# First blocks of x turned by matrix products with a diagonal, and pool matrices multiplied earlier, in a hybrid attention and pooling layer

## The chip, the core and the metric

The kernel runs on one core of a Trainium2 chip. The metric is the device time of one execution in microseconds. The core's engines are TensorE (PE for its products, PEld for its weight loads), VectorE (DVE), ScalarE (ACT), GpSimd (POOL) and SyncE (SP), which here issues almost all DMA transfers. Each engine works through its own instructions in order and waits for the others by semaphores.

## What is computed

One layer of a bidirectional encoder on x of 4096 tokens by 1024 features, in float32:

```python
h = rmsnorm(x, pre_norm_g)
proj = h @ w_in                    # q | k | v | g_a | u_p | g_p
a = banded_attention(q, k, v, rel_bias, sink) * silu(g_a)   # 8 heads, |i-j| <= 128
p = multiscale_pool(u_p, pool_w, pool_scale) * silu(g_p)    # 4 groups of 128 channels
x = x + rmsnorm(concat(a, p) @ w_out, post_norm_g)
```

rmsnorm(x, g) is x / sqrt(mean(x^2) + eps) * g by rows. The pooling takes window means less the token and multiplies each group by a 128x128 matrix of pool_w; since that is linear, the kernel multiplies pool_w into the columns of w_in for u_p beforehand.

## The kernel before

The precision of float32 comes from pairs of float16 numbers: a value's high part, and a low part that is the rest. A product of two pairs is made of three float16 products. Both operands are first scaled: x by its row factor (one over the root of the mean square), a weight tile by a power of two found from its columns' norms.

The kernel has two phases, the projections (lines 200 to 1518) and attention with the output product (from line 1520). In both, every step is put into a list as `due(t, function, arguments)`. A table `later` adds an offset to single steps, the list is sorted by time, and the functions are called in that order. A manual schedule then keeps that order on each engine. So a time is not a start on the chip: it only sets which instruction stands before which in an engine's queue.

The start treats the first 512 tokens by themselves, as four blocks b = 0 to 3 of 128 rows. For each block: `x_load` brings its rows into `ybig`; `x_square` (L245 on ScalarE, L247 on VectorE) makes the sum of squares; `x_scale` (L254, L257 on GpSimd) the row factor; `x_high` (L268, ScalarE) and `x_low` (L275, VectorE) the scaled pair, into `cbig`; `x_turn` (L282) issues a transposing DMA from `cbig` to `xt`, as TensorE needs features on the partitions.

Meanwhile the first weight tiles, 0 and 2 (the gate g_p), are loaded into `raw` and squared (`w_square_raw`, L453, ScalarE). TensorE sums the squares with the squared gains `gg` as weights (`w_norm_raw`, L462; `gg` is from L413 on VectorE). `pair_scale` (L163 to L179) makes the scale. `w_fold` (L416) multiplies the gains into the tile, and `w_high` (L529) and `w_low` (L532) make its pair in `wa`.

`mm_block(si, i)` (L973) multiplies weight tile si with block i, 24 products of 128x128. Later tiles take all 512 tokens at once in `mm` (L985), 24 products each, called a0_1, a0_3, a0_8 and so on after their tile; before a0_8 stands `pair_norm` (L473), a sum of squares for tiles 8 and 10. `u_prod` (L434) multiplies the float32 columns for u_p by a pool matrix, four float32 products for each half, into a PSUM tile named wup, and `u_fold` (L442) multiplies in the gain. `row_prod` (L653) makes the bias table fp. `warm_up` (L955) is a row of products whose result nobody reads.

At the end of the second phase stand the last query blocks, 2, 1 and 0, whose attention, output product and norm alternate on all engines. Steps named below are the logits with their maximum (L1669, DVE), the exponentials (L1680, ACT), the reciprocals of the denominators (L1700, L1701, DVE), the rest of a probability pair (L1731, DVE), the join of a query tile q0_1 (L2021, DVE), and the adds of output products (L2319, DVE, into mo) that free the PSUM bank for TensorE's next product (L2277).

Of the kernel before, what the change touches and what calls it, by code (L numbers as in the profile page):

```python
# [8 lines left out]
F32 = mybir.dt.float32  # L9
F16 = mybir.dt.float16  # L10
BF16 = mybir.dt.bfloat16
# [62 lines left out]
def hybrid_layer(ctx: ExitStack, tc, io, out):  # L74
# [16 lines left out]
    nc.sync.dma_start(g_pre, io["g_pre"])  # L91
# [107 lines left out]
    with ExitStack() as actx:  # L199
# [5 lines left out]
        ones16 = pa1.tile([P, P], BF16, name="ones16")  # L205
# [46 lines left out]
        def x_scale(m, i, n=1):  # L252
            s, r = rs_t[m][:, 0, i : i + n], rs_t[m][:, 1, i : i + n]
            nc.gpsimd.tensor_scalar(  # L254
                out=s, in0=s, scalar1=D * EPS * X_SQ**2, scalar2=None, op0=ALU.add
            )
            nc.gpsimd.tensor_tensor(  # L257
                out=r, in0=s, in1=mhalf if n == 1 else mhalf.to_broadcast([P, n]), op=ALU.pow
            )
# [155 lines left out]
        def w_fold(si):  # L415
            nc.vector.tensor_tensor(out=raw_k(si), in0=raw_k(si), in1=gb, op=ALU.mult)  # L416
# [10 lines left out]
        def u_prod(j, half):  # L427

            wt = raw_of(("u", j))
            pp = psa.tile([P, 4, P], F32, name=f"wup{j}_{half}", tag="wup", bufs=3)  # L430
# [520 lines left out]
        def warm_up():  # L951

            junk = psa.tile([P, 512], F32, name="warm", tag="wup", bufs=3)
            for n in range(6):
                nc.tensor.matmul(junk, ones16, gg[:, :4], start=(n == 0), stop=(n == 5))  # L955
# [196 lines left out]
        for t, b in ((0.0, 0), (0.1, 1), (0.3, 2), (0.4, 3)):  # L1152
            due(t, x_load, b)
        for t, si in ((0.2, 0), (0.25, 2), (9.5, 1), (10.8, 3)):
            due(t, w_load, si, io["w_a"][si])
        due(20.7, lambda: nc.sync.dma_start(pw, io["pool_w"].rearrange("j p c -> p j c")))
        due(20.8, u_load, 0)
        due(20.9, u_load, 2)
        for b, (s, c, h, l) in enumerate(
            ((4.7, 5.95, 7.05, 8.15), (5.95, 7.1, 8.15, 9.4), (11.4, 12.5, 15.0, 16.4),  # L1160
             (12.5, 13.6, 17.3, 18.0))
        ):
            due(s, x_square, b, nc.vector if b == 0 else None)
            due(c, x_scale, 0, b)
# [3 lines left out]
        due(0.5, first_use)  # L1168
        due(2.0, gain_square)
        for si, s, n, f, h, l in (  # L1170
            (0, 9.25, 10.4, 11.2, 13.8, 15.1), (2, 10.3, 11.5, 13.9, 16.1, 18.9),
# [6 lines left out]
        due(12.7, pair_scale, 0)  # L1178
        due(12.9, pair_scaled, 0)
        due(20.9, pair_gate, 0)  # L1180
        due(4.0, row_load)
        due(11.7, row_prod)
        due(11.8, warm_up)
        due(21.0, row_keep)
        due(30.0, row_store)
        for t, si, i in (
            (16.3, 0, 0), (17.7, 0, 1), (19.0, 2, 0), (20.4, 2, 1), (21.7, 0, 2), (23.0, 2, 2),
# [47 lines left out]
        due(20.9, w_fold, 1)  # L1235
        due(22.2, w_square, 1)
        due(22.2, w_fold, 3)
        due(23.5, w_square, 3)
        pair_split(1, 25.0)
        for half in range(2):  # L1240
            due(27.1, u_prod, 0, half)
            due(30.5 + 0.7 * half, u_fold, 0, half)
        t = tile0(1, 29.3)
        t_first(0, 31.9)
        due(32.0, w_square, 8)
        for half in range(2):
            due(t, u_prod, 2, half)
            due(t + 1.9 + 0.7 * half, u_fold, 2, half)
        due(34.7, u_load, 1)
        due(36.4, u_load, 3)  # L1250
        due(38.0, w_square, 10)
        t = tile0(3, t + 1.9)
        t_last(0, 38.0)
        due(37.9, w_fold, 4)
# [9 lines left out]
        due(28.0, w_load_c, 4, 2)  # L1264
        due(29.0, w_load_c, 6, 3)
# [198 lines left out]
        for m in range(1, NM):  # L1464
# [28 lines left out]
            (x_turn, 0, 1): 0.4, (mm_block, 0, 3, 1): 0.8, (t_low, 0, 0, 1): 1.5,  # L1493
            (t_low, 0, 1, 1): 1.5, (t_low, 0, 3, 1): 1.5, (w_square, 4, 1): -1.5,
            (w_fold, 6, 1): -10.0, (u_fold, 1, 0, 1): -0.8, (u_fold, 1, 1, 1): -0.8,
            (u_fold, 3, 0, 1): -0.8, (u_fold, 3, 1, 1): -0.8, (w_fold_act, 12, 0, 1): 0.4,
            (w_fold_act, 13, 0, 2): 6.0, (w_fold_act, 13, 1, 2): 6.0, (q_sums, 'kv', 1): -1.5,
            (q_low, 'kv', 0, 1): 0.15, (q_high, 'kv', 1, 1): -0.8, (w_fold_act, 16, 0, 1): -10.0,
            (out_square, 1, 1): 10.0, (out_square, 4, 1): 10.0, (wo_scale, 4, 1): -0.8,
            (wo_sum1, 0, 1): -3.0, (wo_load, 1, 1): -6.0, (wo_load, 5, 1): -9.0,  # L1500
            (wo_load, 2, 1): 3.0, (wo_load, 6, 1): 3.0, (load_wo, 0, 1): 10.0, (wq_x, 1, 1): -2.2,
            (bias_head, 2, 1): 10.0, (bias_head, 5, 1): 6.0, (bias_head, 6, 1): 6.0,
            (bias_head, 7, 1): 9.0, (bias_sinks, 1): 3.0, (rs_spread, 3, 1): 8.0,
            (x_hi, 2, 'S1', 1): -10.0, (y_scale, 3, 2, 1): 10.0, (rs_row, 4, 1): 1.5,
            (rs_spread, 4, 1): 4.5, (product, 2, 1, 0, 1): -10.0, (x_hi, 4, 'A11', 1): -10.0,
            (rs_row, 5, 1): -0.8, (rs_spread, 5, 1): 5.0, (y_load, 5, 3, 1): 3.0,
            (rs_spread, 6, 1): 8.0, (x_hi, 5, 'S3', 1): -1.5, (y_scale, 6, 0, 1): 3.0,
            (x_hi, 6, 'A11', 1): -0.4, (x_hi, 6, 'A22', 1): -3.8, (x_sum, 'S3', 6): 0.8,
# [1391 lines left out]
```

## Time and profile before

| | us |
|---|---|
| median of 3 runs | 1144.49 (1143.84 to 1144.55) |
| profiled execution, its own time | 1142.67 |
| span of its instructions | 1140.9 |
| PE busy | 1110.8 (97%) |
| DVE busy | 961.1 (84%) |
| ACT busy | 725.0 (64%) |
| POOL busy | 292.5 (26%) |

Times in the profile's rows count from the start of the span. A row of a timeline has the start, the duration, the engine (PEld is the weight load, SPq SyncE's queue of DMA issues), the line of the kernel, the operation with output and input, and in brackets the idle time ahead of it with what ended that. A row of groups has the count, the busy time in total and the mean in ns, and the idle time ahead of the group. The ends of matrix products are modelled, so starts are the safer reading. The time outside the span is 1142.67 - 1140.9 = 1.77 us.

### The profile page before, as it was taken

What the parts mean: (1) busy time and instruction counts of PE and PEld (TensorE: products, weight loads), DVE (VectorE), ACT (ScalarE), POOL (GpSimd) and SP (SyncE); (2) the same over time, 40 slices, a digit from 0 to 9 for tenths busy, and PEclk for the clock granted to TensorE, in tenths of its full rate; (3) what the DMA queues carried; (4) which work ended last, traced back from release to release, by engine and by line L of the source; (5) the groups of instructions that cost most, each with busy time, mean ns of one, the idle gap of its engine ahead of it and who ended that gap; (6) DMA issues with size and microseconds to landing.
All of it is one profiled execution on the core that took longest, in us unless ns stands there. A gap on an engine that the chain in (4) does not pass through costs nothing. (4 is left out here: it accounts for less than half of the span.)

```text
span 1140.9 us, 28920 instructions
## 1 busy us (share of the span) xinstructions
PE 1110.8 (97%) x11556; PEld 816.5 (72%) x11556; DVE 961.1 (84%) x1975; ACT 725.0 (64%) x1625; POOL 292.5 (26%) x280
## 2 busy tenths in 40 slices
PE   5999999999999999999999999999999999999887
PEld 4648888888888888887567657566666666676444
DVE  6878787788878986868998888888888988988996
ACT  5856675757476545166776676676676766776573
POOL 1000000000000000001544454463454545544322
PEclk9999999999999999999999999999999999999999
DMA  9677889899998967999989998889979989889587
GB/s 258 167 252 253 218 229 290 262 262 271 277 281 204 322 217 233 353 265 261 234 203 225 203 212 210 210 187 239 211 188 225 198 192 227 211 206 198 135 187 212
DMA packets 328007, 262.02 MB, mean 230 GB/s; under 512 B 222608, under 2 KB 285712, under 8 KB 324416
## 3 DMA queue, kind: packets, MB, share of 16 engines
q1 hardware_dynamic: 323840, 245.50, 82.2%
q0 software_dynamic: 4032, 14.68, 5.2%
q8 instruction: 90, 1.47, 0.5%
q14 instruction: 45, 0.37, 0.1%
HBM read 130.87 MB, written 76.59 MB: 182 GB/s over the span
## 5 line engine op out<-in xcount | busy, mean ns | idle before, releaser
L1034 PEld LDWEIGHTS <-wa 128*128 128x128 f16 x3360 | 328.1, 98 | 39.4 <-issue 0.8
L1034 PE MATMUL ch<-xt,wa 128*128 128x256 f16 x1920 | 212.6, 273 | 0.0
L1680 ACT ACTIVATE p_all<-p_all,nm 128x385 f32<-128x385 f32 (+1 forms) x256 | 153.0, 599 | 60.8 <-DVE nm L1669 53.1
L1731 DVE SCALAR_TENSOR_TENSOR pn<-p_all,rd,pn 128x384 f16<-128x384 f32 (+1 forms) x256 | 161.5, 681 | 20.1 <-ACT pn L1723 17.4
L2277 PE MATMUL ms<-wa,ys 128*128 128x512 f16 x720 | 165.3, 379 | 2.7 <-DVE mo L2319 1.3
L1669 DVE CUSTOM_DVE_ANT_0 p_all<-s,ybig,nsink 128x385 f32<-128x385 f32 (+1 forms) x256 | 156.9, 664 | 7.1 <-PE s L1652 7.1
L1723 ACT ACTIVATE pn<-p_all,rd 128x384 f16<-128x384 f32 (+1 forms) x256 | 135.4, 596 | 5.5 <-DVE rd L1701 2.9
L2277 PE MATMUL m<-wa,y 128*128 128x512 f16 x540 | 123.9, 379 | 3.7 <-DVE mo L2319 2.1
L2277 PEld LDWEIGHTS <-ys 128*128 128x128 f16 x720 | 69.0, 98 | 79.7 <-issue 5.0
L1034 PE MATMUL cl<-xt,wa 128*128 128x256 f16 x960 | 106.4, 273 | 0.4 <-DVE cbig L1059 0.3
L2277 PEld LDWEIGHTS <-y 128*128 128x128 f16 x540 | 51.2, 98 | 64.4 <-issue 5.7
L254 POOL TENSOR_SCALAR ssq<-ssq 128x4 f32<-128x4 f32 (+1 forms) x11 | 4.0, 362 | 332.4 <-ACT jk L245 326.4
L2157 POOL TENSOR_TENSOR y<-yf,y 128x512 f16<-128x512 f32 x29 | 33.4, 1156 | 201.3 <-ACT y L2153 201.2
L2157 POOL TENSOR_TENSOR ys<-at,ys 128x512 f16<-128x512 f32 x28 | 35.6, 1272 | 131.9 <-ACT ys L2153 131.9
L346 DVE TENSOR_TENSOR xt<-ybig,xt 128x1024 f16<-128x1024 f32 x50 | 60.3, 1219 | 8.2 <-ACT xt L341 8.2
L1926 PEld LDWEIGHTS <-raw 128*128 128x128 f16 x588 | 56.7, 98 | 13.7 <-issue 1.6
L2303 ACT ACTIVATE jkb<-mo 128x512 bf16<-128x512 f32 x42 | 26.3, 626 | 63.1 <-DVE mo L2319 63.1
L1926 PE MATMUL kp<-xt,raw 128*128 128x256 f16 x540 | 65.4, 273 | 0.0
L2314 POOL TENSOR_TENSOR mo<-mo,ybig 128x512 f32<-128x512 f32 x39 | 52.4, 1342 | 44.8 <-ACT jkb L2303 44.6
L1652 PE MATMUL s<-k_all,q 64*32 64x288 f16 (+2 forms) x2856 | 60.2, 284 | 3.4 <-DVE k_all L1898 1.2
L1068 ACT ACTIVATE gp<-cbig,cg 128x256 f32<-128x256 f32 x42 | 19.0, 500 | 62.6 <-DVE cbig L1059 62.6
L1652 PEld LDWEIGHTS <-q 64*32 64x32 f16 (+1 forms) x2856 | 38.4, 92 | 27.1 <-issue 24.6
(248 smaller groups left out, 2025.3 us busy)
## 6 DMA issues: line engine op xcount, KB each, us to landing
xn<-in_x SPq DMA_DIRECT2D x28, 512.0 KB, 9.0
ybig<-in_xT SPq DMA_DIRECT2D x28, 512.0 KB, 5.4
y_scr<-xt SPq DMA_DIRECT2D x14, 1024.0 KB, 8.0
out<-mo SPq DMA_DIRECT2D x28, 512.0 KB, 5.5
xt<-y_scr SPq DMA_DIRECT2D x26, 512.0 KB, 6.2
xt<-in_x POOLq DMA_DIRECT2D x26, 512.0 KB, 4.8
xt<-x_scr SPq DMA_DIRECT2D x19, 512.0 KB, 4.6
x_scr<-xt SPq DMA_DIRECT2D x9, 1024.0 KB, 10.4
```

Source lines behind the costliest of these rows:

```text
L346: eng.tensor_tensor(out=o[:, w, 1], in0=y_view(i), in1=o[:, w, 0], op=ALU.subtract)
L1034: nc.tensor.matmul(acc[:, c], wa[:, q, wi, slot * HK + k, c * P : (c + 1) * P], x[:, xi, k, :], start=(fresh and n == 0), stop=(n > 3 * 2 ...
L1652: nc.tensor.matmul(s_bank[jj][r0 : r0 + nr, gg, lo:hi], q_t[u, half][a, qi, jj, tl + r0 : tl + r0 + nr], k_all[a, ki, k0 : k0 + hi - lo], ...
L1669: nc.vector.tensor_tensor_reduce(out=p_t[b, half][:, hh, :nk], in0=s_t[b, half][jj][:, gg, :nk], in1=bias[:, h, lo : lo + nk], scale=negc[ ...
L1680: nc.scalar.activation(p[:, hh, :nk], p[:, hh, :nk], AF.Exp, bias=nm_t[b, half][:, hh : hh + 1], scale=-1.0, accum_out=den_t[b, half][:, h ...
L1723: nc.scalar.activation(prob_view(b, half)[:, 0, i], p_t[b, half][:, i, :nk], AF.Copy, scale=rd_t[b, half][:, 0, i : i + 1],)
L1731: nc.vector.scalar_tensor_tensor(out=pn4[:, 1, i], in0=p_t[b, half][:, i, :nk], scalar=rd_t[b, half][:, 0, i : i + 1], in1=pn4[:, 0, i], o ...
L1926: nc.tensor.matmul(acc, wkv[:, slot, wi, k, :], x[:, xi, k, :], start=(onto is None and n == 0), stop=(n == 3 * HK - 1), skip_group_check= ...
L2157: eng.tensor_tensor(out=y[:, :, 1], in0=f(u), in1=y[:, :, 0], op=ALU.subtract)
L2277: nc.tensor.matmul(z_t[u, tag], y[:, k, yi, :], wo[o][:, wi, k // 2, k % 2, :], start=(n == 0 and acc is None), stop=(n == 3 * HK - 1), sk ...
L2303: nc.scalar.activation(junk, src, AF.Square, scale=2.0**-5, accum_out=ss_t[u][:, 2 * i + c : 2 * i + c + 1])
L2314: eng.tensor_tensor(out=mo, in0=mo, in1=gpost[:, cs], op=ALU.mult)
```

## The change

Blocks 0 and 1 no longer go through `cbig` and a transposing DMA. GpSimd makes a diagonal matrix of the block's row factors (`x_diagonal`, an identity `eye` times the factors, eye being a new input). TensorE multiplies each 128x128 piece of the block's float32 rows, as weights, by that diagonal (`x_cross`): the product is the piece turned and scaled, in PSUM, in tiles xc0_0, xc0_1, xc1_0, xc1_1 (block and half). ScalarE copies it to `xt` as the high part (`x_cross_high`), VectorE subtracts that for the low part (`x_cross_low`). Blocks 2 and 3 go the old way.

The pool matrices, u0, u2, w1 and w3 are loaded right after x, and the four products for u0 and u2 are made between the block products. The gains g_pre are loaded behind x1 and w0. The warm-up is the first work of TensorE, with 14 products instead of 6, and its operand is a constant instead of gg. The square of block 2 is on VectorE. The bias table is made after a0_3. In the two `later` tables many entries are new or changed.

```diff
+        def x_diagonal(b):
+            d = xc_t["d", b] = pa.tile([P, P], F32, name=f"xd{b}", tag="xd")
+            nc.gpsimd.tensor_scalar(
+                out=d, in0=eye, scalar1=rs_t[0][:, 1, b : b + 1], scalar2=None, op0=ALU.mult
+            )
+
+        def x_cross(b):
+            d = xc_t.pop(("d", b))
+            for half in range(2):
+                acc = xc_t[b, half] = (
+                    gemm.tile([P, 4, P], F32, name=f"xc{b}_{half}", tag="acc0") if b and half
+                    else psa.tile([P, 4, P], F32, name=f"xc{b}_{half}", tag="wup", bufs=3)
+                )
+                for k in range(HK):
+                    c0 = half * 512 + k * P
+                    nc.tensor.matmul(
+                        acc[:, k], ybig[:, b, c0 : c0 + P], d, start=True, stop=True
+                    )
+
+        def x_cross_high(b, half):
+            nc.scalar.copy(x_place(b, half, 0), xc_t[b, half])
+
+        def x_cross_low(b, half):
+            nc.vector.tensor_tensor(
+                out=x_place(b, half, 1), in0=xc_t.pop((b, half)), in1=x_place(b, half, 0),
+                op=ALU.subtract,
+            )
...
         def warm_up():
 
-            junk = psa.tile([P, 512], F32, name="warm", tag="wup", bufs=3)
-            for n in range(6):
-                nc.tensor.matmul(junk, ones16, gg[:, :4], start=(n == 0), stop=(n == 5))
+            junk = gemm.tile([P, T], F32, name="warm", tag="acc2")
+            for n in range(14):
+                nc.tensor.matmul(junk, ones16[:, :P], ones16, start=(n == 0), stop=(n == 13))
...
-        due(20.7, lambda: nc.sync.dma_start(pw, io["pool_w"].rearrange("j p c -> p j c")))
-        due(20.8, u_load, 0)
-        due(20.9, u_load, 2)
+        due(0.5, lambda: nc.sync.dma_start(pw, io["pool_w"].rearrange("j p c -> p j c")))
+        due(0.6, u_load, 0)
+        due(0.65, u_load, 2)
...
-        due(11.7, row_prod)
-        due(11.8, warm_up)
...
+        for n, j in enumerate((0, 2)):
+            for half in range(2):
+                due(17.5 + 0.1 * (2 * n + half), u_prod, j, half, n and half)
+                due(20.2 + 0.7 * (2 * n + half), u_fold, j, half)
+        due(36.0, row_prod)
...
         later = {
+            (x_load, 1, 1): -1.5, (w_load, 0, 1): -0.4, (u_load, 2, 1): 1.5,
```

The following rows are those of the instruction order. First SyncE at the start of the program (raw is a buffer of weights, ybig of x; in_w_uT are the columns for u_p). Before:

```order
L91 DMA g_pre_66<-in_g_pre 128x8
L235 DMA ybig_71<-in_x 128x1024 x2
L400 DMA raw_70<-in_w_a 128x1024 x2
L235 DMA ybig_71<-in_x 128x1024 x2
L647 DMA rbias_126<-in_rel_bias 32x8
L649 DMA onehot_128<-in_onehot 32x512
L400 DMA raw_70<-in_w_a 128x1024
L282 DMA_TRANSPOSE xt_72<-cbig_109 128x16x128 x2
L400 DMA raw_70<-in_w_a 128x1024
L282 DMA_TRANSPOSE xt_72<-cbig_109 128x16x128 x2
L1156 DMA pw_111<-in_pool_w 128x4x128
L400 DMA raw_70<-in_w_uT 128x1024 x2
```

The same place after the change:

```order
L234 DMA ybig_70<-in_x 128x1024
L434 DMA raw_69<-in_w_a 128x1024
L1191 DMA g_pre_66<-in_g_pre 128x8
L234 DMA ybig_70<-in_x 128x1024
L434 DMA raw_69<-in_w_a 128x1024
L1192 DMA eye_113<-in_eye 128x128
L234 DMA ybig_70<-in_x 128x1024 x2
L1195 DMA pw_110<-in_pool_w 128x4x128
L434 DMA raw_69<-in_w_uT 128x1024
L434 DMA raw_69<-in_w_a 128x1024 x2
L434 DMA raw_69<-in_w_uT 128x1024
L316 DMA_TRANSPOSE xt_71<-cbig_108 128x16x128 x2
```

The two transfers that turned blocks 0 and 1 are gone; all loads of the first products, the pool matrices included, stand ahead of the two that turn blocks 2 and 3.

VectorE at the start, from the square of block 0 to the low part of block 3. Before (cbig receives x's low parts, wa the weights'):

```order
L247 ISA jk0_130,ssq0_131<-ybig_71 128x1024
L275 SCALAR_TENSOR_TENSOR cbig_109<-ybig_71,ssq0_131,cbig_109 128x2x512 x2
L416 TENSOR_TENSOR raw_70<-raw_70,g_pre_66 128x1024
L163 TENSOR_REDUCE m2_184<-n2_0_149 128x1
...
L416 TENSOR_TENSOR raw_70<-raw_70,g_pre_66 128x1024
L532 SCALAR_TENSOR_TENSOR wa_73<-raw_70,sc_74,wa_73 128x8x128
L275 SCALAR_TENSOR_TENSOR cbig_109<-ybig_71,ssq0_131,cbig_109 128x2x512 x2
L532 SCALAR_TENSOR_TENSOR wa_73<-raw_70,sc_74,wa_73 128x8x128
```

After the change (xt receives the low parts of the tiles xc):

```order
L450 TENSOR_TENSOR raw_69<-raw_69,g_pre_66 128x1024 x2
L162 TENSOR_REDUCE m2_194<-n2_0_163 128x1
...
L246 ISA jk2_202,ssq0_149<-ybig_70 128x1024
...
L290 TENSOR_TENSOR xt_71<-xc0_0_183,xt_71 128x4x128
L569 SCALAR_TENSOR_TENSOR wa_72<-raw_69,sc_73,wa_72 128x8x128
L290 TENSOR_TENSOR xt_71<-xc0_1_188,xt_71 128x4x128
L290 TENSOR_TENSOR xt_71<-xc1_0_210,xt_71 128x4x128
L290 TENSOR_TENSOR xt_71<-xc1_1_215,xt_71 128x4x128
L569 SCALAR_TENSOR_TENSOR wa_72<-raw_69,sc_73,wa_72 128x8x128
L309 SCALAR_TENSOR_TENSOR cbig_108<-ybig_70,ssq0_149,cbig_108 128x2x512
L450 TENSOR_TENSOR raw_69<-raw_69,g_pre_66 128x1024
```

Both folds and the square of block 2 stand ahead of the first low part, and the low part of block 2 stands behind the second low part of the weights, where it stood ahead of it.

VectorE near the end of the program, at the logits of query block 1, first half (nm1_0), before:

```order
L1669 ISA p_all_5964,nm1_0_16112<-s0_5965,ybig_71,nsink_81,negc_80 128x385
L2021 TENSOR_TENSOR q0_1_16023<-kq2_7_15230,q0_1_16023 128x512
L2319 TENSOR_TENSOR mo2_1_16035<-ms1_2_16036,mo2_1_16035 128x512
...
L1700 RECIPROCAL rd1_0_16114<-den1_0_16113 128x2
L1701 TENSOR_TENSOR rd1_0_16114<-rd1_0_16114,s1_5966 128x2
L1700 RECIPROCAL rd1_0_16114<-den1_0_16113 128x2
```

And after:

```order
L1714 ISA p_all_6000,nm1_0_16148<-s0_6001,ybig_70,nsink_80,negc_79 128x385
L2364 TENSOR_TENSOR mo2_1_16071<-ms1_2_16072,mo2_1_16071 128x512
...
L1745 RECIPROCAL rd1_0_16150<-den1_0_16149 128x2
L1746 TENSOR_TENSOR rd1_0_16150<-rd1_0_16150,s1_6002 128x2
L2066 TENSOR_TENSOR q0_1_16059<-kq2_7_15266,q0_1_16059 128x512
L1745 RECIPROCAL rd1_0_16150<-den1_0_16149 128x2
```

The join of q0_1 left its place ahead of the add and stands between the two pairs of reciprocals.

More of the change, by code (lines that the diff above doesn't have):

```diff
@@ L425, in u_load, with u_prod @@
             raw_load(("u", j), io["w_uT"][j])
-        def u_prod(j, half):
+        def u_prod(j, half, spare=0):
             wt = raw_of(("u", j))
-            pp = psa.tile([P, 4, P], F32, name=f"wup{j}_{half}", tag="wup", bufs=3)
+            pp = (
+                gemm.tile([P, 4, P], F32, name=f"wup{j}_{half}", tag="acc0") if spare
+                else psa.tile([P, 4, P], F32, name=f"wup{j}_{half}", tag="wup", bufs=3)
+            )
             w_t["up", j, half] = pp
@@ L1232, in tile0 @@
             return t + SLOT
[L1235 to L1254, printed above, removed]
+        due(17.0, w_fold, 1)
+        due(19.6, w_square, 1)
+        due(18.2, w_fold, 3)
+        due(21.7, w_square, 3)
+        pair_split(1, 23.0)
+        due(24.5, w_square, 8)
+        due(27.0, w_square, 10)
+        t = tile0(1, 27.1)
+        t_first(0, 29.0)
+        due(31.0, u_load, 1)
+        due(31.1, u_load, 3)
+        t = tile0(3, t)
+        t_last(0, 34.0)
+        due(34.9, w_fold, 4)
         due(t + 1.3, w_square, 4)
@@ L1515, in hybrid_layer @@
-            (join, 7, 1, 'a', 'u2', 0, 1, 1): -1.5,
+            (pool_gate, 7, 0, 1): -0.8, (pool_store, 7, 1, 1): -1.5,
+            (join, 7, 0, 'a', 'u2', 0, 1, 1): -1.9, (join, 7, 1, 'a', 'u2', 0, 1, 1): -1.5,
         }
@@ L2888 @@
         "edge": _edge_table().reshape(64),
+        "eye": np.eye(P, dtype=np.float32),
     }
```

124 lines of the change are left out of this document (72 added, 52 removed).

## The prediction

> **What bounds the kernel now.** I first read the busy shares by stage. Each row gives the stretch, its length and the busy time of PE, PEld, DVE, ACT and POOL, with the number of instructions.
>
> ```profile
> 0.00:17.00 17.00, 6.34 (x26) 2.77 (x26) 10.61 (x18) 11.87 (x15) 4.39 (x12) 1.00 0.94 285
> 48.00:1055.00 1007.00, 1002.31 (x10575) 750.69 (x10574) 855.51 (x1761) 645.63 (x1456) 264.49 (x245) 1.00 0.90 233
> 1055.00:1141.00 86.00, 72.26 (x650) 39.18 (x648) 71.58 (x157) 47.83 (x124) 23.31 (x23) 0.98 0.71 179
> ```
>
> In the middle stretch TensorE idles 1007.00 - 1002.31 = 4.7 us out of a thousand. Nothing that only reorders VectorE, ScalarE or SyncE there can win more than that, and the diff leaves nearly all of it alone. So two questions remain: when does the product stream reach the middle, and how do the 13.7 idle us of the last stretch change? Next I read whom TensorE waits for (total, times, longest).
>
> ```profile
> PE n L462 <- ACT sq L453: 10.7, 1, 10.7
> ...
> PE gp L973 <- DMA xt<-cbig: 1.1, 1, 1.1
> ```
>
> Its start is a wait of 10.7 us for the first squared weights, and a second wait, of 1.1 us, is for the turned blocks 2 and 3. TensorE's own timeline (start, duration) shows what lies between:
>
> ```profile
> 10.66 1.96 PE L462 MATMUL n<-sq,gg 128*128 128x128 bf16 x16 [10.66 <-ACT sq L453]
> 12.55 1.87 PE L653 MATMUL fp<-onehot,rbias 32*8 32x512 f32 x2
> 14.36 2.74 PE L955 MATMUL warm<-gg,ones 128*128 128x512 bf16 x6
> 16.89 5.90 PE L973 MATMUL gp<-xt,wa 128*128 128x128 f16 x96
> 23.90 2.84 PE L973 MATMUL gp<-xt,wa 128*128 128x128 f16 x48 [1.11 <-DMA xt<-cbig]
> ...
> 29.46 2.05 PE L434 MATMUL wup<-pw,raw 128*128 128x128 f32 x16
> 31.34 5.34 PE L985 MATMUL a<-xt,wa 128*128 128x512 f16 x24
> 36.53 1.95 PE L434 MATMUL wup<-pw,raw 128*128 128x128 f32 x16
> ...
> 43.49 0.28 PE L473 MATMUL n<-wsq,ones 128*128 128x2 f32 x2
> ...
> 47.50 5.34 PE L985 MATMUL a<-xt,wa 128*128 128x512 f16 x24
> ```
>
> The first product of weight tile 8, a0_8, starts at 47.50. Both programs issue the same list from there on, so the front is worth exactly what that start moves. Two prices come from these rows. The warm-up products take (16.89 - 14.36) / 6 = 0.42 us for 512 columns; those of a0_1 take (36.53 - 31.34) / 24 = 0.216. TensorE therefore begins at half rate, and has full rate from about 17 us.
>
> **The loads.** The queue rows and the first work on x show how loads arrive.
>
> ```profile
> 0.73 0.40 SPq L91 DMA_DIRECT2D g_pre<-in_g_pre  x1
> 1.18 0.89 SPq L235 DMA_DIRECT2D ybig<-in_x  x2
> ...
> 17.61 6.03 SPq L282 DMA_TRANSPOSE xt<-cbig  x2
> ```
>
> ```profile
> 5.09 1.23 DVE L247 CUSTOM_DVE_ANT_0 jk<-ybig 128x1024 bf16<-128x1024 f32 x1 [1.44 <-DMA ybig<-in_x]
> ```
>
> ```profile
> 6.37 1.06 ACT L245 ACTIVATE jk<-ybig 128x1024 bf16<-128x1024 f32 x1 [4.15 <-DMA ybig<-in_x]
> ```
>
> Blocks 0 and 1 of x are released 1.28 us apart: one 512 KB block per 1.28 us, in order of issue. Without g_pre ahead the first block goes out at 0.73 instead of 1.18. By that spacing I estimate x1 at 4.6, w0 5.9, x0 7.2, w2 8.45, eye 8.6, x2 9.9, x3 11.1, pool matrices 11.8, u0 13.0, u2 16.9.
>
> **The work ahead of the products.** These rows carry the prices of VectorE, ScalarE and GpSimd:
>
> ```profile
> 10.98 1.22 DVE L416 TENSOR_TENSOR raw<-raw,g_pre 128x1024 f32<-128x1024 f32 x1
> 12.66 0.42 DVE L163 TENSOR_REDUCE m<-n 128x1 f32<-128x256 f32 x1 [0.46 <-PE n L462]
> ...
> 13.68 0.17 DVE L179 TENSOR_SCALAR sc<-m 128x2 f32<-128x2 f32 x1
> ...
> 16.30 1.28 DVE L275 SCALAR_TENSOR_TENSOR cbig<-ybig,ssq,cbig 128x1024 f16<-128x1024 f32 x1
> ```
>
> ```profile
> 6.74 0.57 POOL L257 TENSOR_TENSOR ssq<-ssq,mhalf 128x1 f32<-128x1 f32 x1
> ```
>
> ```profile
> L1046 ACT COPY cbig<-ch 128x512 f32<-128x512 f32 x60 | 34.1, 578 | 21.9 <-PE ch L1034 21.8
> ...
> L2157 POOL TENSOR_TENSOR y<-yf,y 128x512 f16<-128x512 f32 x29 | 33.4, 1156 | 201.3 <-ACT y L2153 201.2
> ...
> L529 ACT ACTIVATE wa<-raw,sc 128x1024 f16<-128x1024 f32 x10 | 11.3, 1138 | 1.4 <-DVE sc L179 1.4
> ...
> L442 DVE TENSOR_TENSOR raw<-wup,g_pre 128x512 f32<-128x512 f32 x8 | 5.3, 685 | 0.2
> ```
>
> ScalarE squares w0 and then w2, 1.0 us each, from 8.45 for the second; TensorE can sum them (n2_0) from 9.5 to 10.6. VectorE takes gain square at 5.95, block 0's square to 8.4, two gain folds of 1.22 to 10.8, the scale chain of 1.2 us (12.66 to 13.85 before) to 11.9, then the square of block 2 that came over from ScalarE, to 13.1. GpSimd had block 0's factor 7.31 - 6.32 = 1.0 us after its square, so now at 9.35. The diagonal is a 128x128 operation that the trace does not show. It lies between nothing and the 1.16 us of the four times larger L2157; even the upper end gives 10.5, before TensorE is free of n2_0, so it costs nothing.
>
> The turning products replace two transfers: 16 fp32 products of 128x128. The eight of L434 take 31.34 - 29.46 = 1.88, so 0.235 each and 3.8 us for all: TensorE is in them from 10.6 to 14.4. The copy out of PSUM (like L1046, 0.58) and the subtraction (like L442, 0.69) come four times each, in between the high and low parts of the weights (1.14 and 1.28). Following both queues: ScalarE has x high parts out at 12.2, 14.9, 15.4, 17.1, w0's high part from 13.25 to 14.4, w2's to 16.5. VectorE waits for 14.4, gives w0's low part at 15.6, the x low parts at 13.9, 16.2, 16.9, 17.7, w2's low part at 18.95.
>
> TensorE, from 14.4: one pool product (0.94) to 15.35, x low of block 0 is late only to 16.2, so the two 24s of weight tile 0 with a second pool product between run to 19.6; a third to 20.55, the 48 of weight tile 2 (2.85) to 23.4, the fourth to 24.35. The gate projection of blocks 0 and 1 ends 0.6 us later than before (22.79), but with all four pool products done.
>
> **The wait that is left.** Blocks 2 and 3 still go through the low part and the queue. VectorE reaches x_low of block 2 after w2's low part: 18.95 to 20.2, where it was 16.30 to 17.6. That is the late step of this change: 2.6 us. The transfer was issued at 17.61 and released TensorE at 23.90. Medians from issue to landing, and a spread with most samples, are:
>
> ```profile
> xt<-cbig SPq DMA_TRANSPOSE x4, 6.2
> ```
>
> ```profile
> vv<-vt SPq DMA_TRANSPOSE x14, 5.8
> ```
>
> ```profile
> DMA to landing us min/median/max: 4.3/6.5/10.4
> ```
>
> The third is that of wa<-pn. With the two transfers of blocks 0 and 1 gone, and fewer loads beside (w1, w3 and u are in by 17), I take 5.8, the row of single turns; bounds 4.3 and 6.5. Products of block 2 then start at 26.0 (24.5 to 26.7), a wait of 1.65 us for TensorE, where 1.1 was. All of TensorE's list queues behind that wait. On SyncE the loads of the bias table, w4, w6, u1 and u3 queue behind the two turns. The bias table is used from 41.95 on. u3 is wanted by the last pool products, at an estimated 45; it went out at 40.73 before,
>
> ```profile
> 40.73 0.33 SPq L400 DMA_DIRECT2D raw<-in_w_uT  x1
> ```
>
> when VectorE had the second low part of weight tile 1's sums. That chain now starts from n2_1 some 2 us later, but has lost four pool folds of 0.69 in between, so I keep 40.7 and take nothing; it leaves an estimated 4.3 us for the landing.
>
> Blocks 2 and 3 take 29.46 - 23.90 = 5.56, so a0_1 starts at 31.55 (31.34 before). Its weights' high part follows n2_1, at 28.85, by a chain of 1.2 and a copy of 1.14: 31.2, with 0.35 to spare. The two a0 take 5.19 each, to 41.95. The bias table's product, which was paid at half rate (1.87), now stands behind them at full rate: 0.94. Then 47.50 - 43.49 = 4.0 for the row sum and four pool products as before: **a0_8 at 46.9, or -0.6 us**, bounds -2.1 (landing after 4.3) and +0.1 (after 6.5).
>
> In short, the front hides 3.8 us of pool products and 2.5 of warm-up, saves 0.9 on the table and pays 3.8 for turning; what else it frees waits for VectorE, late with block 2.
>
> **The tail.** The last list of offsets moves few instructions. One stood on TensorE's path:
>
> ```profile
> 1081.50 0.68 DVE L2021 TENSOR_TENSOR q<-kq,q 128x512 f16<-128x512 f32 x1
> 1082.10 0.68 DVE L2319 TENSOR_TENSOR mo<-ms,mo 128x512 f32<-128x512 f32 x1
> ...
> 1085.41 0.17 DVE L1700 RECIPROCAL rd<-den 128x2 f32<-128x2 f32 x1 [0.57 <-ACT p_all L1680]
> ```
>
> ```profile
> 1082.84 2.75 PE L2277 MATMUL ms<-wa,ys 128*128 128x512 f16 x12 [1.35 <-DVE mo L2319]
> ```
>
> TensorE's 1.35 ends with the add of L2319, and the q join stood right ahead of it. It goes behind the first of the reciprocals, in the 0.57 us that VectorE waits there anyway: -0.6. ScalarE's square of a finished block leaves the middle of block 1's exponentials, after which VectorE waited 0.19: -0.2. The other swaps exchange neighbours in stretches where TensorE's next wait is set elsewhere; I take nothing for them, bounds -0.35 (ScalarE's four products of the last but one block, now ahead of a copy) and, the other way, if the q join's time is only paid later, at the reciprocals, the whole -0.8. **Tail: -0.8**, bounds -1.15 and 0.
>
> **Sum.** -0.6 - 0.8 = -1.4 us. The profiled execution took 1142.67 with a span of 1140.9; the runs had a median of 1144.49, 1.8 above it. The difference carries over: 1143.1.
>
> **Rivals.**
>
> *The turn is quick (F).* Only two turns are left in the queue, and the shortest landing of a turn was 4.3. Then the wait before block 2 all but goes, a0_8 starts at 45.4, and with the tail it is -2.1 - 0.8 = -2.9: 1141.6. Against it: the four of this very shape have 6.2 as their median. By the Trainium skill (DMA: Bandwidth & Descriptors, Latency and other measured facts) a DMA transpose moves 261 GB/s on top of about 2 us fixed; for the 512 KB of a block that is an estimate of 4.0 us, which would give this case. The row of 6.2 does not agree, with other transfers beside it.
>
> *The clock falls back (C).* The warm-up now ends near 7.1 us, and TensorE stands idle to 9.5. If the half rate of 0.42 comes back there, n2_0 still ends by 11.5, but turning takes 7.5 us, to 19, the last copy comes at 18.8, w2's and block 2's low parts at 21.9 instead of 20.2, block 2 is turned at 27.7 and a0_8 starts at 48.6: +1.1, to +1.5 with the pool products also slow. With the tail's gain at its lower bound that is 1145.6 to 1146.0, slower; with the whole of it 1144.8. It decides from the point where x_cross takes over 0.35 us a product. For it: before, the rate was half until 17 us although TensorE worked from 10.66 on. Against it: 14 products are 5.9 us without a gap, about as long as from 10.66 to 16.89, after which the rate was full. By the Trainium skill (TensorE: Matmul & The Clock Gate, Part 1: The HAM clock gate) one idle window of about 3.4 us returns the array to half rate; the gap here is an estimated 2.4 us, so by that rule the case does not come, if barely.
>
> *The change moves the work, not the time (N).* The wait before block 2 takes all that the front sets free (landing 6.5: +0.1), and the q join's 0.6 is paid again where VectorE next sets TensorE's pace. Then 1144.3 to 1144.6. For it: VectorE is busy 71.58 of the last 86 us.
>
> **How the numbers follow.** My forecast has 0.45, F 0.25, C 0.12, N 0.18. A measurement of this kernel can tell about 0.2% from no change, 2.3 us. F is beyond that with most of its chance, and the forecast's own lower end reaches it: faster 0.29. C stays within it unless more goes wrong than the clock, which I leave 0.09 for slower. Same: 0.62. The range: F below with its further bound (-2.1 and -1.15, and 0.4 for the spread of runs) 1140.8; C above, 1145.6.
>
> **What would show it.** Right: VectorE's first square of x ends near 8.4, n2_0 near 10.6, x_cross takes 0.235 a product, x_low of block 2 ends near 20.2, TensorE waits some 1.6 us for the turned block 2, a0_8 starts near 46.9; the 1.35 before ms falls to about 0.75. Wrong: a0_8 before 46 (the turn or the loads are quicker), or after 48 (the clock; or u2 later than 19.6 or u3 later than 45, since all later products stand behind those two in TensorE's queue); or waits in the tail that were not there.

## The result, and the profile after

| | before | after |
|---|---|---|
| median of 4 runs, us | 1144.45 | 1152.53 (1151.32 to 1152.9) |
| profiled execution, us | 1142.67 | 1152.48 |
| span, us | 1140.9 | 1150.7 |
| a0_8 starts at | 47.50 | 48.73 |
| row sum of weight tiles 5 and 7 starts at | 73.67 | 79.63 |
| first pg product, the first for the next 512 tokens (L1094 before, L1131 after) | 89.35 | 98.47 |
| last group of ms products | 1109.36 | 1119.12 |

The change made the kernel slower, by a ratio of 1.007 (95% interval 1.0052 to 1.0087). The forecast was 1143.1, with at most 1145.6 in its range.

TensorE's waits after the change (total, times, longest):

```profile
PE n L510 <- ACT wj L506: 4.6, 1, 4.6
...
PE n L499 <- ACT sq L490: 2.3, 1, 2.3
PE xc L278 <- POOL xd L265: 1.8, 1, 1.8
...
PE cl L1071 <- DVE u L1096: 1.6, 1, 1.6
```

The wait of 10.7 us at the start is gone, and so is the wait for the turned blocks 2 and 3. A new one of 4.6 us stands in a place of which the prediction says nothing. TensorE's timeline of the changed kernel:

```profile
7.41 0.61 PE L499 MATMUL n<-sq,gg 128*128 128x128 bf16 x8
10.33 0.61 PE L499 MATMUL n<-sq,gg 128*128 128x128 bf16 x8 [2.31 <-ACT sq L490]
12.74 6.16 PE L278 MATMUL xc<-xd,ybig 128*128 128x128 f32 x32 [1.81 <-POOL xd L265]
...
27.88 2.84 PE L1010 MATMUL gp<-xt,wa 128*128 128x128 f16 x48
...
33.43 10.52 PE L1022 MATMUL a<-xt,wa 128*128 128x512 f16 x48
...
48.73 5.34 PE L1022 MATMUL a<-xt,wa 128*128 128x512 f16 x24
```

```profile
79.63 0.59 PE L510 MATMUL n<-wsq,ones 128*128 128x2 f32 x2 [4.56 <-ACT wj L506]
80.08 18.56 PE L1022 MATMUL a<-xt,wa 128*128 128x512 f16 x72
```

The 72 products behind the gap took 18.56 us. The same 72 before:

```profile
73.81 15.70 PE L985 MATMUL a<-xt,wa 128*128 128x512 f16 x72
```

The windows of the changed kernel (PE, PEld, DVE, ACT, POOL, then the granted clock) show why, and show the same for the turning products:

```profile
7.40:10.80 3.40, 1.09 (x17) 0.92 (x15) 2.86 (x4) 1.06 (x1) 1.49 (x2) 1.00 1.01 393
10.80:17.60 6.80, 4.99 (x26) 4.86 (x23) 3.64 (x11) 2.75 (x5) 5.63 (x9) 0.50 0.91 346
17.60:79.10 61.50, 57.47 (x445) 36.41 (x444) 47.65 (x83) 38.62 (x59) 1.28 (x2) 1.00 0.65 161
79.10:85.90 6.80, 6.27 (x16) 2.52 (x17) 4.49 (x10) 4.46 (x7) 0.00 (x0) 0.50 0.51 197
```

So the 9.8 us of the span come in four parts. The front to a0_8 gives +1.23. From there to the row sum of tiles 5 and 7 comes the stall: 79.63 - 73.67 = 5.96, less 1.23, is +4.7. The half clock behind it brings the shift to 98.47 - 89.35 = 9.12, another +3.2. Further on it rises to 11.3 by 990 us (the wait of 1.6 for a PSUM bank at 152 us is the largest piece), and the tail takes 1.5 off again, to 9.8. The medians differ by 8.1 only: the profiled execution of the kernel before (1142.67) lay 1.8 below its median, for a reason that the record does not show.

**What was late for the row sum.** Follow it back: the sum waits for the square of tile 7 on ScalarE, that for the gain fold on VectorE, that for the load of w7 (the rows of weight tile 7; w5 is the same for tile 5). The fold before the change and after it:

```profile
70.99 1.23 DVE L416 TENSOR_TENSOR raw<-raw,g_pre 128x1024 f32<-128x1024 f32 x1 [1.36 <-DMA raw<-in_w_a]
```

```profile
77.12 1.23 DVE L450 TENSOR_TENSOR raw<-raw,g_pre 128x1024 f32<-128x1024 f32 x1 [2.97 <-DMA raw<-in_w_a]
```

SyncE's queue there, of the kernel before:

```profile
49.02 0.38 SPq L311 DMA_DIRECT2D rs_scr<-ssq  x1
52.12 0.33 SPq L400 DMA_DIRECT2D raw<-in_w_a  x1
52.49 9.44 SPq L325 DMA_DIRECT2D ybig<-in_xT  x4
62.03 1.99 SPq L400 DMA_DIRECT2D raw<-in_w_a  x1
```

And of the changed one:

```profile
55.50 0.39 SPq L345 DMA_DIRECT2D rs_scr<-ssq  x1
55.95 0.49 SPq L434 DMA_DIRECT2D raw<-in_w_a  x1
56.53 11.22 SPq L359 DMA_DIRECT2D ybig<-in_xT  x4
67.85 1.84 SPq L434 DMA_DIRECT2D raw<-in_w_a  x1
```

The first row of each is the store of the row factors of the next 512 tokens, 2 KB in pieces of 4 bytes. It went out 6.5 us later, and with it everything behind it: w5 (3.8 us later), four loads of the transposed x, and w7 (5.8 us later). Behind the store the queue moves little, in both kernels. In the ten microseconds after it the core moves 25 GB/s (last number), against 264 from 66 to 72:

```profile
56.00:66.00 10.00, 10.00 (x49) 4.72 (x48) 8.27 (x18) 5.21 (x9) 0.00 (x0) 1.00 0.90 25
```

```profile
66.00:72.00 6.00, 6.00 (x30) 2.74 (x28) 2.81 (x3) 3.40 (x4) 0.00 (x0) 1.00 0.82 264
```

The store waits for GpSimd's row factors, and those for the squares of blocks 4 to 7 on ScalarE (jk4 to jk7; the loads of their rows are xn4 to xn7). The last two, jk6 and jk7, stood here before:

```profile
44.28 1.05 ACT L245 ACTIVATE jk<-xn 128x1024 bf16<-128x1024 f32 x1
...
46.35 1.04 ACT L245 ACTIVATE jk<-xn 128x1024 bf16<-128x1024 f32 x1
```

and stand here after the change, jk6 behind the high parts of weight tiles 8 and 10 and the square of 9, jk7 also behind the squares of 6 and 11 (the middle row is the square of 6):

```profile
49.62 1.04 ACT L244 ACTIVATE jk<-xn 128x1024 bf16<-128x1024 f32 x1
...
51.84 1.06 ACT L506 ACTIVATE wj<-raw 128x1024 bf16<-128x1024 f32 x1
...
52.89 1.04 ACT L244 ACTIVATE jk<-xn 128x1024 bf16<-128x1024 f32 x1
```

The reason lies in the times of the plan. The loads and squares of these rows have fixed dates (`x_loads(1, (27.0, 33.0), (28.0, 35.0), (36.0, 42.0), (37.0, 44.0))`) that the change leaves as they were. The weight tiles' dates count from each other, and the change moved them: `tile0(1, 29.3)` became `tile0(1, 27.1)` and the pool products' 1.9 behind it went, so tile 8 has the date 41.7 instead of 45.8. Two chains that had been dated to fit slid 4.1 past each other.

### The profile page after: what moved, and what is told of

Read it like the earlier page. It is cut to its first block, busy times and chain, and to the rows that moved or that the text cites. A ratio compares the mean times of both kernels' runs of the same rounds, so it can differ in the third digit from the quotient of the medians.

```text
span 1150.7 us, 29011 instructions
## 1 busy us (share of the span) xinstructions
PE 1121.4 (97%) x11596; PEld 824.4 (72%) x11596; DVE 962.3 (84%) x1979; ACT 724.0 (63%) x1625; POOL 295.8 (26%) x282
## 5 line engine op out<-in xcount | busy, mean ns | idle before, releaser
L1776 DVE SCALAR_TENSOR_TENSOR pn<-p_all,rd,pn 128x384 f16<-128x384 f32 (+1 forms) x256 | 161.9, 683 | 19.5 <-ACT pn L1768 17.6
L1971 PEld LDWEIGHTS <-raw 128*128 128x128 f16 x588 | 56.8, 98 | 13.6 <-issue 1.6
```

The lines of the kernel that those rows point to most:

```text
L1776: nc.vector.scalar_tensor_tensor(out=pn4[:, 1, i], in0=p_t[b, half][:, i, :nk], scalar=rd_t[b, half][:, 0, i : i + 1], in1=pn4[:, 0, i], o ...
L1971: nc.tensor.matmul(acc, wkv[:, slot, wi, k, :], x[:, xi, k, :], start=(onto is None and n == 0), stop=(n == 3 * HK - 1), skip_group_check= ...
```

## The experiments

Each run stands beside runs of the kernel before on its own chip; those medians lie between 1142.29 and 1142.67, below the 1144.45 above. Differences are therefore given against the kernel before of the same set.

**1. The rows early again.** The first and the second edit ask whether that order is the cause, and which part of the chain holds the loads.

```diff
-        x_loads(1, (27.0, 33.0), (28.0, 35.0), (36.0, 42.0), (37.0, 44.0))
+        x_loads(1, (27.0, 31.0), (28.0, 33.0), (31.05, 38.0), (31.06, 40.0))
```

> The changed kernel, with one edit: the loads and squares of the next 512 rows (blocks 4 to 7, jk4 to jk7) get dates about 4 earlier, so that they again stand ahead of the squares and high parts of weight tiles 8 to 11 on ScalarE, as in the kernel before. Theory: ScalarE reached jk7 at 52.9 instead of 46.4, GpSimd's row factors and with them the small store rs_scr followed at 55.5 instead of 49.0, and on SyncE the loads of w5 and w7 stand behind that store; TensorE then waits 4.6 us for the row sum of tiles 5 and 7 and runs 2.9 us longer at half rate behind the gap. By that the store goes out near 49.5, w7 near 62.5, the 4.6 us wait and the second stretch at half clock are gone, and the time falls by 7 to 8 us, to about 1145. Rival, that the loads are late because the queue is full with other data (the pool loads moved to the front, the two turns behind them): the store moves, but w7 lands no more than 1 or 2 us earlier and half of the wait stays: 1150.

Measured: 1144.27, ratio to the kernel before 1.001 (1.000 to 1.0019), so +1.6 us where the whole change had +8.1. The store went out at 50.45 and w7 at 61.74; the wait of 4.6 us is gone and the clock stays at full rate behind the row sum. From a0_8 to the first pg product this run loses nothing against the kernel before, where the change loses 7.9. The gain is 6.5 where 7 to 8 was expected, since a new wait took its share: u3, a load of columns for u_p, now stands behind xn6 and xn7 on SyncE.

```profile
PE wup L471 <- DMA raw<-in_w_uT: 1.3, 1, 1.3
```

**2. The store behind the loads.**

```diff
         later = {
+            (rs_row, 1, 1): 14.0,
```

> The changed kernel, with one edit: the small store of the row factors (rs_scr of macro block 1) is moved in SyncE's queue from ahead of the loads of w5, the transposed x and w7 to behind them; ScalarE's order stays as changed. Theory: it is this store, waiting for jk7, that holds the loads. Then w5 goes out near 53.6, w7 near 65 or earlier, w7 lands before 73 and TensorE's 4.6 us wait is gone or under 1 us, the time about 1145 to 1147, with perhaps a new wait at the spread of the row factors, which now comes later. If the full queue were the cause, w7 would still land near 76 and the wait stay.

Measured, in one run: 1142.24 (the kernel before: 1142.67). ScalarE's order is that of the change, but SyncE's queue reads:

```profile
53.32 0.35 SPq L434 DMA_DIRECT2D raw<-in_w_a  x1
53.72 2.11 SPq L359 DMA_DIRECT2D ybig<-in_xT  x4
58.28 0.34 SPq L434 DMA_DIRECT2D raw<-in_w_a  x1
58.72 0.42 SPq L345 DMA_DIRECT2D rs_scr<-ssq  x1
...
69.99 0.33 SPq L349 DMA_DIRECT2D rb<-rs_scr  x1
```

w7 goes out 9.6 us earlier than in the change, even 3.8 earlier than before it, and TensorE waits for nothing at the row sum. The four loads of x are issued in 2.11 us instead of 11.22. From a0_8 to the first pg product it loses nothing against the kernel before. The load that reads the stored factors back goes out 69.99 - 58.72 = 11.3 us behind the store; that is not the store's time alone, since five loads of 512 KB still stood ahead of it. So it was the store, late and ahead of the loads, and not the amount of data. No wait for the spread appeared.

**3. TensorE kept busy at the start**, on top of run 1.

```diff
+        due(7.85, keep_up, 10)     # unread products of 512 columns
+        due(8.95, keep_up, 8)
```

> The kernel of the first run here, with 10 more unread products of 512 columns between the two halves of n2_0 and 8 more ahead of the turning products. Theory: the granted clock fell to half at 10.8 us because TensorE idled 2.3 and 1.8 us around n2_0; with it busy the turning products take 3.8 us instead of 6.0, and a0_8 starts 1 to 2 us earlier (near 47.3 instead of 48.7), the time 1 to 2 us below the first run. Rival: fp32 products with a moving diagonal cost 0.375 us each whatever the clock; then nothing changes but the added products.

Measured: 1143.68, ratio 1.0011 (0.9996 to 1.0025), 0.6 below run 1, whose interval it overlaps. In the trace the effect is plain; the turning products of both blocks, in this run:

```profile
12.95 2.05 PE L278 MATMUL xc<-xd,ybig 128*128 128x128 f32 x16
15.47 2.05 PE L278 MATMUL xc<-xd,ybig 128*128 128x128 f32 x16 [0.48 <-POOL xd L265]
```

From 15.47 to the next product at 17.36 is 0.236 us for each of eight, as forecast, where the change took (18.73 - 12.74) / 16 = 0.374. The granted clock is 1.00 from 7.4 to 17.6. Block 2's products start 0.91 earlier, at 27.05 instead of 27.96 in run 1. That is what VectorE's first low part gained, which waits for ScalarE's copy of the first turned half: 14.76 instead of 15.66. a0_8 starts at 48.15 instead of 50.40, as run 1's wait of 1.3 for u3 has gone too; but of these 2.25 us only 0.7 are left by 1000 us, the first piece going to a wait of 1.1 us for a PSUM bank at 144 us.

**4. The tail alone**: the kernel before with only the second phase's offsets of the change.

> The kernel before, with only the second phase's table of offsets from the change. Theory: the last blocks gain about 1.0 us (TensorE's wait for the add falls from 1.35 to about 0.7), so 1143.5 against 1144.45; the forecast had 0.8. Rival: the swaps cost as much elsewhere as they give, no difference.

Measured: 1141.11, ratio 0.9984 (0.9973 to 0.9996), so -1.6 us. TensorE's wait for the add fell from 1.35 to 0.75, and a wait of 0.83 for the reciprocals went too. After the change:

```profile
1093.54 2.75 PE L2322 MATMUL ms<-wa,ys 128*128 128x512 f16 x12 [0.75 <-DVE mo L2364]
```

The wait before the last ms products rose, but a wait of 0.59 for a transposing transfer just ahead of it (at 1107.78 before) went, so that the way from the last o products to these ms products is 0.2 shorter after the change. Before and after:

```profile
1109.36 2.75 PE L2277 MATMUL ms<-wa,ys 128*128 128x512 f16 x12 [0.41 <-DVE xt L2319]
```

```profile
1119.12 2.75 PE L2322 MATMUL ms<-wa,ys 128*128 128x512 f16 x12 [0.97 <-DVE xt L2364]
```

**5. The folds behind the scale chain**, on top of run 2.

```diff
-            (0, 6.7, 7.8, 7.9, 11.0, 12.2), (2, 7.8, 8.9, 9.0, 13.3, 14.5),
+            (0, 6.7, 7.8, 9.1, 11.0, 12.2), (2, 7.8, 8.9, 9.15, 13.3, 14.5),
```

> The changed kernel with the small store behind the loads (as in the run before it), and one more edit: VectorE's gain folds of weight tiles 0 and 2 stand behind the scale chain instead of ahead of it, so that VectorE is idle while GpSimd makes the first row factor. Theory: GpSimd's two small operations took 1.13 and 1.52 us instead of 0.23 and 0.57 because VectorE ran the folds at that time. Then they take 0.23 and 0.57 again, the diagonal is ready near 10.1 instead of 12.7, turning begins right behind n2_0 near 11.0, and turns block 2 about 0.5 us earlier (VectorE still has the same sum of work ahead of x_low): a0_8 near 48.1 instead of 48.65. Rival: GpSimd waits for something else (the landing of eye, its first instructions' loading); then they stay at 1.1 and 1.5 us.

GpSimd in the change, while VectorE ran the two folds (9.05 to 11.53):

```profile
9.22 1.13 POOL L253 TENSOR_SCALAR ssq<-ssq 128x1 f32<-128x1 f32 x1 [8.79 <-DVE ssq L246]
10.44 1.52 POOL L256 TENSOR_TENSOR ssq<-ssq,mhalf 128x1 f32<-128x1 f32 x1
```

and in this run, with VectorE free of the folds:

```profile
9.34 0.23 POOL L253 TENSOR_SCALAR ssq<-ssq 128x1 f32<-128x1 f32 x1 [8.91 <-DVE ssq L246]
9.66 0.57 POOL L256 TENSOR_TENSOR ssq<-ssq,mhalf 128x1 f32<-128x1 f32 x1
```

The diagonal is ready at 10.96 instead of 12.69, turning starts at 11.24, and a0_8 at 47.60, a gain of 1.05 where 0.5 was expected. GpSimd was held up by VectorE's folds: from run 2, where the two operations took 1.13 and 1.53 and the diagonal was ready at 12.73, the place of the folds is all that differs. The Trainium skill (SBUF — State Buffer, SBUF: two separate sides) says that an operation of VectorE with two inputs in SBUF locks a port pair that GpSimd needs, for its whole length. These rows agree. In one run the time was 1142.72, not below run 2: of the gain at a0_8 0.2 are left at 480 us, where TensorE now waits 1.1 us for VectorE.

**6. The square of block 2 back on ScalarE, and 10 unread products** between the halves of n2_0, on top of run 5.

```diff
+        due(7.85, keep_up, 10)
...
-            due(s, x_square, b, None if b > 2 else nc.vector)
+            due(s, x_square, b)
```

> The run before it, with 10 unread products between the halves of n2_0 and the square of block 2 back on ScalarE, which is idle there. Theory: what sets the front is VectorE's sum of work before x_low of block 2, then 4.6 us of landing; without the 1.2 us square, x_low of block 2 ends near 21.5 instead of 23.2, its products start near 26.1 instead of 27.8 and a0_8 near 46.9, below the 47.5 of the kernel before. Rival: ScalarE, now with the square, is late with the high part of w0 and VectorE waits for that; then no more than 0.5 us.

Measured, in one run: 1140.46, that is -1.8. Block 2's products start at 25.83 and a0_8 at 46.68, as expected. The time lies below all 15 runs of the kernel before in this set (1140.65 to 1145.59). Neither of the two edits was run alone on run 5, so their shares are not known.

**7. One offset of the first phase taken out**, on top of run 6.

```diff
-            (rs_spread, 3, 1): 8.0, (pool_tile, 0, 2, 1): -0.8,
+            (rs_spread, 3, 1): 8.0,
```

> The run before it, with one offset of the first phase's table taken out, (pool_tile, 0, 2): -0.8, which had put five VectorE operations of the pooling ahead of the add that frees a PSUM bank at 152 us. Theory: TensorE's wait of 1.6 us for that add goes, and the kernel is the fastest of all: the tail's 1.0, the front's 0.6 and no stall, against 1142.67 before about 1140.5 to 1141. Rival: the wait only moves to another step behind, no difference to the run before it.

Measured: 1140.10, ratio 0.9978 (0.9969 to 0.9988), -2.2 us: a version faster than both kernels. But the reason given fell. Its products run ahead of those of run 6 by 0.58 us at a0_8 and 0.40 at the end. The lead comes from the first 11 us, where both kernels have the same instructions and only the loads landed at other times; so run 7 is not told apart from run 6. The wait for a PSUM bank (1.6 us at 152 us in the change) is 1.1 in run 3, 0.3 in run 2 and gone in run 6, all of them with the offset. So the offset alone does not make that wait, and what does was not followed up. Nor is all of the -2.2 the front's: run 4, with the tail alone, had -1.6 in its set, which leaves the front some 0.6, while the trace has a0_8 1.4 earlier than before. The front of this version:

```profile
10.93 3.84 PE L278 MATMUL xc<-xd,ybig 128*128 128x128 f32 x32
...
25.24 2.84 PE L1016 MATMUL gp<-xt,wa 128*128 128x128 f16 x48 [0.30 <-DMA xt<-cbig]
...
46.10 4.26 PE L1028 MATMUL a<-xt,wa 128*128 128x512 f16 x19
```

**8. Blocks 0 and 1 turned the old way**, on top of run 2: pairs in cbig and transposing transfers, with the new loads, pool products and warm-up.

```diff
-            due(s + 1.25, x_diagonal, b)
-            due(t, x_cross, b)
...
+            due(h, x_high, b)
+            due(l, x_low, b)
+            due(u, x_turn, b)
```

> The changed kernel with the small store behind the loads, but blocks 0 and 1 turned as in the kernel before, by scaled pairs and transposing transfers; the early loads, the early pool products and the early warm-up stay. Theory: turning on TensorE is what costs the front its 3.8 to 6.0 us and frees the queue; four transfers in a row then land about 2.3 us apart, the first issued near 10.3, and blocks 2 and 3 come no later than with the change: a0_8 between 47 and 49, the time within 1.5 us of the second run of the first set. If turning on TensorE is worth its 3 us, a0_8 comes at 50 or later.

Measured: 1149.07, ratio 1.0057 (1.0042 to 1.0072), 6.8 us slower. The first wait is:

```profile
PE gp L1010 <- DMA xt<-cbig: 5.9, 1, 5.9
```

The first transfer, issued at 10.95, landed after 9.4 us, where the two of run 1 took 4.6 and 4.9. Its issue alone held SyncE for 7.4 us, so that the second, for which TensorE waited, went out at 18.41. The loads of w1, w3 and u2 stand ahead of the first in the queue. Meanwhile TensorE fell to half rate (0.66 from 18 to 30 us). Blocks 2 and 3 follow 4.8 us later than in run 2, and a0_8 starts at 53.44, not at the 47 to 49 expected. So with this order of loads turning on TensorE is worth its price; that the loads ahead delay the transfer was not tried by itself.

**9 and 10. The two halves of run 1**: only the squares' dates earlier, and only the loads'.

```diff
+        x_loads(1, (27.0, 31.0), (28.0, 33.0), (36.0, 38.0), (37.0, 40.0))   # 9
+        x_loads(1, (27.0, 33.0), (28.0, 35.0), (31.05, 42.0), (31.06, 44.0)) # 10
```

> The changed kernel with only the squares jk4 to jk7 earlier in ScalarE's order; the dates of the loads of those rows stay as changed. Theory: ScalarE's order alone put the store 6.5 us late, since xn7 (out at 43.8) had landed long before jk7 at 52.9. Then the store goes out near 50.5 as in the first run, the stall of 4.6 us is gone, and u3, no longer behind xn6 and xn7 on SyncE, costs no 1.3 us either: 1143 to 1144. Rival: it was the late loads of xn6 and xn7; then jk7 still comes after 51, and the time stays above 1148.

> The other half: the changed kernel with only the loads of those rows earlier, ScalarE's order as changed. Theory: no gain; the store still goes out at 55 or later, the wait for the row sum of tiles 5 and 7 stays at 4 us or more, and u3, behind xn7, adds up to 2 us: 1152 to 1155. Rival (the loads): 1145.

Measured: run 9 1146.97, ratio 1.004 (1.0025 to 1.0055), and run 10, once, 1152.19. Neither half is enough. In run 9 the square stands early on ScalarE, but its rows are not there:

```profile
48.91 1.06 ACT L244 ACTIVATE jk<-xn 128x1024 bf16<-128x1024 f32 x1 [3.03 <-DMA xn<-in_x]
```

ScalarE waits 3.03 us, and what is queued behind, the high part of tile 8, then holds a0_8 for 2.1 us; the store goes out at 54.70. The wait at the row sum is gone, but a0_8 itself starts at 52.19, 4.7 later than before. So my theory that ScalarE's order alone was at fault was too narrow: loads and squares have to move together. In run 10 the store went out at 58.98 and the wait of the row sum stayed, at 3.0 (u3 had already cost 3.3).

**11. The front's three edits without the store's**: runs 5 and 6 on the change itself.

> The changed kernel with the three edits of the front (folds behind the scale chain, 10 unread products between the halves of n2_0, the square of block 2 on ScalarE) and with the small store where the change has it, ahead of the loads of w5 and w7. Theory: the front and the stall are separate; a0_8 starts near 46.1 to 46.7 instead of 48.7, but ScalarE's order still puts jk7 behind wj11, the store some 6 us after where the kernel before had it relative to a0_8, and TensorE's wait for the row sum of tiles 5 and 7 stays at 4 us or more with a stretch at half clock behind it: about 1150. Rival: the stall came from the late front; with a0_8 earlier than before the wait falls under 2 us: 1145 or less.

Measured: 1146.44, ratio 1.0032 (1.002 to 1.0043), +4.1. a0_8 starts at 46.11, and still:

```profile
PE n L510 <- ACT wj L506: 4.5, 1, 4.5
```

The wait and the half clock behind it stay: from a0_8 to the first pg product this run loses 7.5 us against the kernel before. Front and stall are two separate things. The time was 3.6 lower than expected. Of that 2.1 is the kernel before, whose median is 1142.37 in this set and not 1144.45; against it, 5.5 was expected and 4.1 measured. The rest is that the front was worth more than its 2.6 us at a0_8: behind the place of the wait of 1.6 us for a bank, which was gone, the lead on the change had grown from 3.05 to 4.76 us.

## Why the prediction was wrong

**The step that failed** is the first: "In the middle stretch TensorE idles 1007.00 - 1002.31 = 4.7 us out of a thousand. [...] and the diff leaves nearly all of it alone", and "Both programs issue the same list from there on, so the front is worth exactly what that start moves." The second sentence holds for TensorE's list, of which it was said. It does not hold for ScalarE and SyncE. That TensorE waited for nothing there before says that its suppliers were in time, not how much they had to spare. It could have been read from the trace of before: ScalarE's square of tile 7 ended at 73.45 (the row that reads out its sum), and TensorE took the row sum at 73.67.

```profile
73.26 0.19 ACT L469 ACTIVATION_READ_ACCUMULATOR wj<-raw 128x1 f32 x1
```

```profile
73.67 0.28 PE L473 MATMUL n<-wsq,ones 128*128 128x2 f32 x2
```

So that chain had 0.2 us to spare, on an engine that was busy 64% of the time, and any delay of w7 beyond that came through. The sizes fit: the fold of w7 came 77.12 - 70.99 = 6.1 later; less the 0.2 to spare and the 1.2 by which TensorE itself was late, that is the 4.7 of the stall. Runs 1, 2 and 11 show the cause: the loss of 7.9 us from a0_8 to the first pg product, stall and clock, is gone with either edit of the order (1 and 2), and stays, at 7.5, with the front's edits alone (11).

**The front**: forecast -0.6 at a0_8, measured +1.23. Four steps of the sum came late; the landing, below, went the other way.
- The loads of block 0 and w2 were taken to land so that their squares start near 7.2 and at 8.45; they came 0.7 and 0.8 later (block 0 in run 7 too, at 7.93):

```profile
7.90 1.23 DVE L246 CUSTOM_DVE_ANT_0 jk<-ybig 128x1024 bf16<-128x1024 f32 x1 [0.80 <-DMA ybig<-in_x]
```

```profile
9.22 1.06 ACT L490 ACTIVATE sq<-raw 128x1024 bf16<-128x1024 f32 x1 [2.48 <-DMA raw<-in_w_a]
```

- The diagonal was to be ready by 10.5 at the worst; it came at 12.69. Its own 0.62 lay inside the bounds. The two small operations ahead of it were taken at their length before, 1.0 us together, and took 2.7, since the change put VectorE's folds beside them (run 5).
- Turning was priced at 0.235 a product and took 0.374: rival C, in part. Run 3 shows that it was the clock. The gap was judged "an estimated 2.4 us, so by that rule the case does not come, if barely"; it measured 2.31 (8.02 to 10.33), and yet the rate had fallen at 10.8, before the second gap of 1.81 began. The rule of the Trainium skill (TensorE: Matmul & The Clock Gate, Part 1: The HAM clock gate) speaks of an idle window of about 3.4 us; here TensorE was busy for 1.09 of the 3.4 us from 7.4 to 10.8, and that was idle enough. The second gap goes with the length of the half rate: 6.8 us in the change, 3.4 in run 5, which has a first gap of 2.74 and no second (0.50 from 10.2 to 13.5, 1.00 from 13.6 to 17).
- x_low of block 2 was to end at 20.2 and ended at 23.26, mostly as a consequence of these. It ends at 22.14 in run 5, with the folds moved, at 21.18 in run 6, with the clock kept and block 2's square off VectorE as well, and at 20.62 in run 7.

**The landing** went the other way. The forecast took 5.8; in run 1 TensorE, waiting, was released 27.96 - 23.34 = 4.6 us after the issue: rival F's mechanism was right. It saved 1.2 us of the loss above: 3.06 later with x_low, less 1.2, is 48.73 instead of 46.9. Rival C has a0_8 at 48.6, near the measured time, and that is in part luck: it has x_low at 21.9 and a landing of 5.8. With the front repaired (run 7) a0_8 starts at 46.10, earlier than the forecast's 46.9 by the landing less an x_low that is still 0.4 late.

**The tail** was right in its mechanism, and larger: -0.8 forecast, -1.6 in run 4. The wait for the add fell to 0.75, as written; of the wait of 0.83 for the reciprocals the sum had only the 0.2 of ScalarE's square.

**The range** took its upper end from the clock alone. All rivals looked at the front, the turn and the tail; none at what a shift of dates does to steps with fixed dates. The time above the range is the 7.9 us of the middle stretch, for which the sum had nothing.

## What to carry to other kernels

Where order comes from a table of times, look for the entries that did not move: if one group's dates are relative and another's absolute, an edit of the first reorders both, on every engine. Before calling a stretch safe because the busiest engine never waits there, follow its suppliers one and two steps back and write down by how much each is early. In this kernel the small scattered store belonged behind the loads that matter in the same queue, and gaps in TensorE of 2.3 us and more cost their length and then 3.4 to 6.8 us at half clock.

## What the runs showed of the hardware

- A store of 2 KB as 512 pieces of 4 bytes held up the queue behind it for about 10 us: 25 GB/s in that time in the change, and in the kernel before it landed 10.1 us after its issue. With the store behind them (run 2), the four loads of x were issued in 2.11 instead of 11.22 us.
- GpSimd's operations of 0.23 and 0.57 us took 1.13 and 1.52 beside VectorE's float32 folds (run 5 against the change and run 2).
- The granted clock fell to 0.50 at 10.8 us, after a gap of 2.31; with a second gap of 1.81 behind it for 6.8 us, without one (run 5) for 3.4. It fell again 4.0 us into the gap of 4.56, for 6.8 us. Ten unread products in the first gap kept it at 1.00 (run 6).
- A transposing transfer of 512 KB landed in 4.6 us in run 1, when the core had moved little in the 3 us before (5 GB/s), and in 9.4 in run 8, where three loads were issued in the 4 us before. That the loads are the reason was not tried by itself.
